# The first part of a down projection as seven products, moved into the gate-up stage

## The chip, the cores and the metric

The kernel runs on one NeuronCore of one Trainium2 chip. Such a core has a matrix engine (TensorE, PE in the profile; its weight loads are shown apart as PEld) and three engines for elementwise work: VectorE (DVE), ScalarE (ACT) and GpSimd (POOL). SyncE (SP) issues the DMA transfers. Each engine works through its own list of instructions in order and waits on semaphores for the others. SBUF is the memory on the chip with 128 partitions; PSUM takes the results of matmuls, in banks.

The metric is the device time of one execution in microseconds. The time before is 1231.87 us, the median of three runs (1230.77 to 1232.3).

## The reference, cut to what matters

Two layers work on 512 prompt positions and 64 sample positions, 576 columns in all, of model width 1024. The first mixes tokens by a convolution module, the second by stick-breaking attention. After each stands the same feed-forward block:

```python
D_FF = -(-8 * D_MODEL // (3 * 256)) * 256          # 2816 = 22 tiles of 128

def swiglu(xn, w_gu, w_down):
    g, u = jnp.split(xn @ w_gu, 2, axis=-1)
    return (jax.nn.silu(g) * u) @ w_down

    h = h + mix                                    # or the attention's output
    h = h + swiglu(rmsnorm(h, ffn_norm_g[l]), ffn_w_gu[l], ffn_w_down[l])
```

All is in float32. The outputs are the normalised stream, the convolution's states, and the keys and values.

## The kernel before, in words

**Products in three matmuls.** Each float32 operand is split into a high part in a rounded format and a low part (the rest). A product is made of three matmuls into one PSUM bank: high by high, high by low, low by high. The 576 columns are worked on as two halves of 288, so the unit of PE's work is a matmul of 128x128 weights with 128x288 operands.

**Weights.** A raw weight tile comes by DMA into one of four places (`wr0` to `wr3`). ACT writes its high part (`wh`) and also a copy of that in a PSUM bank (`hp`), and DVE subtracts that copy from the weights to get the low part (`wl`, L520). A piece has at most 512 columns, that is four blocks of 128, and lives in one of six slots (`N_W`). A slot comes free when its last matmul is done.

**Seven products for eight.** Most of the block is computed two output tiles at a time, in the Strassen-Winograd manner: two output tiles, the two halves of the contraction and the two halves of the columns make a 2x2 by 2x2 block product, for which seven block products are enough. `fast` lists the weights for it as seven pieces: 1, 2 and 4 are raw blocks, 7, 6, 5 and 3 are sums of raw blocks, made by POOL into one of four places `S` (L440 and L476; 5 is made on the way to 6 and used as a piece too). `operands` (L1318 on) makes the other side: for each pair of contraction tiles four sums (`ta`: L1357, L1360; `tb`: L1364, L1367), by the engines in `T_ENG`, and the high (ACT L1335) and low (DVE L1339) parts of these and of the raw halves. In the names, `('a', 0, 1)_2_tb` is layer 0, part 1, pair of columns 2, second sums. `run_jobs` issues the products (PE L1424) in the order of `FAST` = 7, 1, 6, 4, 2, 5, 3 for two pairs of output tiles at once, into three PSUM banks for each (A, B, C). After each product a piece of result is taken out of the bank.

**The feed-forward block** (`ffn`) has 22 tiles of the inner width. Gate-up: tile 0 is computed plainly, tile 1 by seven products alone, and tiles 2 to 21 in pairs, each pair by `run_jobs` over the normalised input's operands (`xops`). What comes out is copied by ACT (L1572) or added by DVE (L1578); POOL scales both results (L1601), ACT takes silu (L1605) and DVE multiplies (L1607). That leaves the tile `a`. Down: the contraction over 22 tiles is cut into three parts, `DK` = tiles 0 to 5, 6 to 13, 14 to 21, each added to the residual `h`. The first part is plain: `plain_operands` splits six tiles `a` (ACT L1626, DVE L1630), and for eight output tiles twelve products each run in `pd` (L596, `add_h` L751). The second and third part are seven-product jobs over `PAIRS` of output tiles, with operands from `a_operands`, and DVE adds each piece of result to `h` (L1693).

**What sets the order.** Nothing of this is written out in the order in which it runs. Each step is handed to a `Plan` as an operation with its engine, its cost and the tiles that it reads and writes. For each section of the program a list scheduler then places all operations on the engines, by the longest chain of work behind each, and the result of several rounds back and forth with the shortest end is emitted. Operations on POOL, and those on DVE that are marked `port` (both inputs in SBUF), are placed so that they don't overlap. A whole feed-forward block is one section. `prepare_operands` hands on the operands' steps one tile at a time, as long as there are places for them in SBUF (`spots`: `x` places, 36 `f` places and a few `k` places); `give` returns a place.

Of the kernel before, what the change touches and what calls it, by code (L numbers as in the profile page):

```python
# [3 lines left out]
F32 = mybir.dt.float32  # L4
# [84 lines left out]
DK = ((0, 6), (6, 14), (14, 22))  # L89
PAIRS = ((0, 4), (1, 5), (2, 6), (3, 7))  # L90
# [13 lines left out]
T_ENG = ("Pool", "Pool", "Pool", "Pool")  # L104
# [115 lines left out]
def build(tc, xT, vec, st, stp, bdp, wt, ck, cv, w_in, w_out, gu, down, wk, wv, wq, wo, yT, csp, css, kp, ks, vp, vs):  # L220
# [45 lines left out]
    def ffn_srcs(l):  # L266
# [1039 lines left out]
    def spot_tile(key, tag, dt=F32):  # L1306
        return tile(key, tag, (P, T), dt, pool=xpool if tag[0] == "x" else None)
# [151 lines left out]
    def ffn(l, mixer, g_next, nrm_next, x_busy, k_busy):  # L1459
# [153 lines left out]
        atags, adeps = [], {}  # L1613

        def plain_operands():

            for m in range(*DK[0]):
                yield 2
                tags_ = [single(), single()]
                atags.extend(tags_)  # L1620
                k = ("ap", l, m)

                def hi(m=m, k=k, tags_=tags_):
                    X[("at", l, m)] = ts = [spot_tile(k + (q,), t, F32R) for q, t in enumerate(tags_)]
                    X[k] = by_half(ts)
                    nc.scalar.activation(ts[0], X[("a", l, m)], AF.Copy)  # L1626

                def lo(m=m):
                    a, b = X[("at", l, m)]
                    nc.vector.tensor_tensor(b, X[("a", l, m)], a.bitcast(F32), op=ALU.subtract)  # L1630

                keys = [by_part(t) for t in tags_]
                op("ACT", act(T, False), hi, reads=by_part(at[m]), writes=keys[0] + keys[1])
                op("DVE", dve(T), lo, reads=by_part(at[m]) + keys[0], writes=keys[1], port=True)
                adeps[k] = keys[0] + keys[1]
                give(at[m])
# [38 lines left out]
        for m in range(2, NF, 2):  # L1675
            evacs = []
            finish = [gate_up(q, evacs) for q in (m, m + 1)]
# [3 lines left out]
            run_jobs(xops, evacs, m == NF - 2)  # L1681
            for f in finish:
                f()
        prepare_operands(force=True)
        table("natural_log_exp_and_others")

# [15 lines left out]
        for g in range(3):  # L1702
            if g < 2:
                a_operands(g + 1)
            if not g:
                for i, m in enumerate(ORDER):
                    tag = (("b0", "b1"), ("b2", "b3"), ("b4", "b5"))[i % 3]
                    prepare_operands()
                    wi, k = take(), ("pd", l, m, 0)
                    newps(k, tag)  # L1710
                    mm_ops(k, tag, wi, [("ap", l, q) for q in range(*DK[0])], xdeps=adeps.get)
                    add_h(m, k, tag)
                for t in atags:
                    give(t)
            for prs in (PAIRS[:2], PAIRS[2:]) if g else ():
# [755 lines left out]
```

## Time and profile before

One execution was profiled. Its span is 1229.2 us, while the timed runs gave 1230.77 to 1232.3 us.

| What | Value |
|---|---|
| timed runs, median | 1231.87 us |
| profiled execution, span | 1229.2 us |
| PE busy | 1204.8 us (98%), 8934 instructions in the trace |
| DVE busy | 978.2 us (80%) |
| ACT busy | 980.3 us (80%) |
| POOL busy | 766.2 us (62%) |
| HBM read | 105.18 MB |
| seven-product work on PE (L1424) in the chain of waits | 29% (A), 14% (B), 7% (C) of the span |
| `pd` (L596), the plain first part, in the chain of waits | 7% |

How to read it: an engine's busy time is the time in which it had an instruction under way. The chain of waits goes back from the last instruction to what released it, step by step, and says on which engine the span was spent. In groups of instructions a row shows line, engine, operation, the tile written and the tiles read, the shapes and the count, and then busy time in us and the mean length of one in ns; behind that comes the idle time ahead of them and what ended it. The first parts lie at about 463 to 505 us (layer 0) and 1087 to 1126 us (layer 1).

### The profile page before, as it was taken

The page shows a single profiled execution, that of the slowest core. Times are in us where ns is not written, and L with a number is a line of the kernel's source. Part 1 is how long each engine was busy: PE and PEld are TensorE (multiplying, and loading weights), DVE is VectorE, ACT ScalarE, POOL GpSimd, SP SyncE. Part 2 cuts the span into 40 slices and gives each one's busy share as a digit, 9 for nine tenths or more (in the row PEclk, how much of TensorE's full clock was granted, in tenths as well). Part 3 has the DMA queues.
Part 4 walks back from the last instruction along what each step waited for, and adds up shares of the span by engine and source line. Part 5 has one row for each costly group of instructions (what it writes and reads, how often), then busy time and mean ns, then how long its engine had stood idle before and what let it go on. Part 6 is the DMA issues. An engine that isn't in the chain of part 4 may idle for free.

```text
span 1229.2 us, 24245 instructions
## 1 busy us (share of the span) xinstructions
PE 1204.8 (98%) x8934; PEld 1185.0 (96%) x8934; DVE 978.2 (80%) x1599; ACT 980.3 (80%) x1877; POOL 766.2 (62%) x636
## 2 busy tenths in 40 slices
PE   9999989999999999999999999998999999999996
PEld 8999989999999999999999999998999999999996
DVE  6999977967665569886788999999866566699965
ACT  7998475698887888687678999956988888896873
POOL 1999824469767758855214555554877768677631
PEclk9999999999999999999999999999999999999999
DMA  7233822133232333223372232232232232332222
GB/s 270 86 93 97 263 71 73 52 115 93 87 121 69 104 86 104 87 82 106 111 202 62 52 83 65 53 103 69 70 123 84 87 119 71 98 108 83 92 69 78
DMA packets 44999, 121.10 MB, mean 99 GB/s; under 512 B 8784, under 2 KB 14224, under 8 KB 44880
## 3 DMA queue, kind: packets, MB, share of 16 engines
q1 hardware_dynamic: 44880, 119.56, 32.3%
q8 instruction: 70, 1.15, 0.4%
q14 instruction: 49, 0.40, 0.1%
HBM read 105.18 MB, written 5.70 MB: 90 GB/s over the span
## 4 chain that ended last, share of the span: by engine, by line
PE 81%; DVE 8%; ACT 1%; issue 1%; DMA 0%; POOL 0%; DVEq 0%; ACTq 0%
PE j_A L1424 29%; PE j_B L1424 14%; PE pd L596 7%; PE j_C L1424 7%; PE pq L596 4%; PE b L2206 4%; PE po L596 4%; PE pw L596 2%; PE b L2142 2%; PE b L2234 2%; DVE acc L1057 2%; PE pg L596 1%; PE pv L1957 1%; DVE wl L520 1%; PE pk L596 1%; DVE xs L1524 1%
## 5 line engine op out<-in xcount | busy, mean ns | idle before, releaser
L510 ACT ACTIVATE wh<-wr 128x512 fp32r<-128x512 f32 (+1 forms) x303 | 183.8, 612 | 36.9 <-PE po L596 15.2
L520 DVE TENSOR_TENSOR wl<-wr,hp 128x512 fp32r<-128x512 f32 (+1 forms) x241 | 158.6, 662 | 53.1 <-ACT hp L515 52.1
L520 DVE TENSOR_TENSOR wl<-S,hp 128x512 fp32r<-128x512 f32 x226 | 152.4, 680 | 40.6 <-ACT hp L515 37.7
L510 ACT ACTIVATE wh<-S 128x512 fp32r<-128x512 f32 x228 | 141.2, 627 | 31.9 <-PE pd L596 10.5
L515 ACT ACTIVATE hp<-wr 128x512 fp32r<-128x512 f32 (+1 forms) x241 | 139.0, 579 | 24.5 <-DVE wl L520 21.7
L515 ACT ACTIVATE hp<-S 128x512 fp32r<-128x512 f32 x226 | 134.0, 596 | 11.9 <-POOL S L440 6.9
L440 POOL TENSOR_TENSOR S<-wr,wr 128x512 f32<-128x512 f32 x57 | 76.5, 1341 | 93.0 <-ACT wh L510 31.0
L1074 POOL TENSOR_TENSOR pacc<-pacc,pr 128x608 f32<-128x608 f32 x69 | 108.9, 1592 | 7.9 <-ACT pr L1071 4.7
L476 POOL TENSOR_TENSOR S<-wr,S 128x512 f32<-128x512 f32 x57 | 78.8, 1385 | 30.2 <-DVE wl L520 17.3
L440 POOL TENSOR_TENSOR S<-wr 128x512 f32<-128x512 f32 x57 | 78.0, 1370 | 26.9 <-DVE wl L520 9.6
L440 POOL TENSOR_TENSOR S<-S,wr 128x512 f32<-128x512 f32 x57 | 77.2, 1354 | 14.4 <-DVE wl L520 7.1
L1601 POOL TENSOR_TENSOR a<-a,r 128x576 f32<-128x576 f32 x44 | 66.8, 1521 | 15.7 <-DVE a L1578 15.7
L1601 POOL TENSOR_TENSOR t<-t,r 128x576 f32<-128x576 f32 x44 | 65.8, 1497 | 9.4 <-ACT t L1572 8.1
L596 PE MATMUL pd<-ap,wh 128*128 128x288 f32 x384 | 66.0, 294 | 0.0
L1057 DVE SCALAR_TENSOR_TENSOR acc<-u,vecs,acc 128x608 f32<-128x608 f32 x76 | 64.5, 849 | 1.0
L1071 ACT ACTIVATE pr<-u,vecs 128x608 f32<-128x608 f32 x69 | 54.2, 797 | 8.1 <-POOL pacc L1074 7.8
L1607 DVE TENSOR_TENSOR a<-a,t 128x576 f32<-128x576 f32 x44 | 49.6, 1127 | 9.0 <-ACT t L1605 8.5
L596 PEld LDWEIGHTS pd<-ap,wh 128*128 128x128 f32 x384 | 56.0, 188 | 0.0
L520 DVE TENSOR_TENSOR wl<-wr,wh 128x512 fp32r<-128x512 f32 x62 | 49.7, 812 | 6.4 <-ACT wh L510 6.3
L1572 ACT ACTIVATE t<-j_A 128x288 f32<-128x288 f32 x84 | 34.0, 406 | 22.3 <-PE j_A L1424 21.5
L1693 DVE TENSOR_TENSOR h<-j_A,h 128x288 f32<-128x288 f32 x60 | 27.1, 453 | 19.6 <-PE j_A L1424 19.3
L1578 DVE TENSOR_TENSOR t<-j_C,t 128x288 f32<-128x288 f32 x42 | 19.1, 455 | 29.0 <-PE j_C L1424 28.9
(857 smaller groups left out, 4504.7 us busy)
## 6 DMA issues: line engine op xcount, KB each, us to landing
wr<-gu SPq DMA_DIRECT2D x88, 512.0 KB, 3.6
wr<-down SPq DMA_DIRECT2D x32, 512.0 KB, 3.7
wr<-w_in SPq DMA_DIRECT2D x15, 512.0 KB, 3.7
wm<-wt SPq DMA_DIRECT2D x12, 576.0 KB, 5.4
wr<-down SPq DMA_DIRECT2D x16, 384.0 KB, 3.2
qd<-qd SPq DMA_DIRECT2D x21, 256.0 KB, 3.0
wr<-w_out SPq DMA_DIRECT2D x8, 512.0 KB, 3.6
wr<-wq SPq DMA_DIRECT2D x8, 512.0 KB, 3.7
```

The source lines that it names most:

```text
L440: eng(e).tensor_tensor(t[:, :n], x[1](), y[1](), op=ALU.subtract if sub else ALU.add)
L476: eng(e).tensor_tensor(v[:, :n], X[("raw", i0)][:, n : 2 * n], v[:, :n], op=ALU.subtract)
L510: nc.scalar.activation(X[("w", u)][0][:, :n], get(), AF.Copy)
L515: nc.scalar.activation(t[:, :n], get(), AF.Copy)
L520: eng(le).tensor_tensor(b[:, :n], get(), a.bitcast(F32)[:, :n], op=ALU.subtract)
L596: nc.tensor.matmul(o[hf], (hi, hi, lo)[j][:, s], (xh, xl, xh)[j], start=(start and q == 0 and j == 0), stop=(stop and q == n - 1 and j == ...
L1057: nc.vector.scalar_tensor_tensor(dst, src, wt_, dst if i else X[("kneg",)], op0=ALU.mult, op1=ALU.add)
L1071: nc.scalar.activation(tile(("pr", c, i), f"pr{m}", (P, YW)), src, AF.Copy, scale=wt)
L1074: nc.gpsimd.tensor_tensor(X[("pacc", c)], X[("pacc", c)], X[("pr", c, i)], op=ALU.add)
L1424: nc.tensor.matmul(out, a[:, s], b, start=(start and q == 0 and i == 0), stop=(q == len(ops_) - 1 and i == 2), skip_group_check=True,)
L1601: nc.gpsimd.tensor_tensor(X[k], X[k], r, op=ALU.mult)
L1607: op("DVE", dve(T), lambda: nc.vector.tensor_tensor(X[ku], X[ku], X[kg], op=ALU.mult), reads=by_part(tg), writes=by_part(tu), port=True)
```

## The change

The down projection's first part is computed as seven products for two output tiles at a time, like the other two parts. It no longer stands behind the gate-up stage: when the pair of tiles 8 and 9 is done (`MID` = 10), the operands of tiles 0 to 5 are made, with their sums on DVE for this part, and the part's four pairs of output tiles follow, ahead of gate-up tiles 10 and 11. The weights' loads move with it in the list of sources. The plain path (`plain_operands`, the loop over `pd`) is gone. From tile 18 on (`AHEAD`), the operands of the second part are handed on between the gate-up pairs, as far as a reserve of places allows (two, and one more for each tile that is still to come). `down_evac` and `finished` only stand earlier.

```diff
+MID = 10
+AHEAD = 18
-T_ENG = ("Pool", "Pool", "Pool", "Pool")
+T_ENG = (("DVE", "DVE", "DVE", "DVE"), ("Pool", "Pool", "Pool", "Pool"), ("Pool", "Pool", "Pool", "Pool"))
...
         for m in range(2, NF, 2):
+            if m == MID:
+                a, b = DK[0]
+                for prs in PAIRS[:2], PAIRS[2:]:
+                    fast([[down[l, q][:, a * P : b * P] for q in p] for p in prs], (b - a) // 2)
             fast([(gu[l, q], gu[l, q + NF]) for q in (m, m + 1)], 4)
-        a, b = DK[0]
-        for m in ORDER:
-            direct(down[l, m][:, a * P : b * P], (b - a) * P)
...
-        def plain_operands():
...
-            todo_.append((operands(aops[g], ("a", l, g), ts, T_ENG, ("xf", "xf", "fx")[g], l == 1 and g == 2), 0))
+            todo_.append((operands(aops[g], ("a", l, g), ts, T_ENG[g], ("fx", "xf", "fx")[g], l == 1 and g == 2), 0))
...
         for m in range(2, NF, 2):
+            if m == MID:
+                a_operands(0)
+                prepare_operands(force=True)
+                for prs in PAIRS[:2], PAIRS[2:]:
+                    run_jobs(aops[0], [down_evac(p) for p in prs], prs == PAIRS[2:])
             evacs = []
             finish = [gate_up(q, evacs) for q in (m, m + 1)]
-            if m == NF - 2:
-                todo_.append((plain_operands(), 0))
-                prepare_operands()
+            if m == AHEAD:
+                a_operands(1)
+            if m >= AHEAD:
+                prepare_operands(2 + NF - 2 - m)
             run_jobs(xops, evacs, m == NF - 2)
             for f in finish:
                 f()
...
-        for g in range(3):
+        for g in (1, 2):
             if g < 2:
                 a_operands(g + 1)
-            if not g:
-                for i, m in enumerate(ORDER):
-                    tag = (("b0", "b1"), ("b2", "b3"), ("b4", "b5"))[i % 3]
-                    prepare_operands()
-                    wi, k = take(), ("pd", l, m, 0)
-                    newps(k, tag)
-                    mm_ops(k, tag, wi, [("ap", l, q) for q in range(*DK[0])], xdeps=adeps.get)
-                    add_h(m, k, tag)
-                for t in atags:
-                    give(t)
-            for prs in (PAIRS[:2], PAIRS[2:]) if g else ():
+            for prs in (PAIRS[:2], PAIRS[2:]):
```

Three places show how the instructions stand. In the rows a number behind a name tells the buffers of one name apart; lines of the changed kernel are 3 higher than before.

On PE before, in layer 0, where the last gate-up products end and the plain first part begins:

```order
L1424 MATMUL j_A<-('x', 0, 3)_0_b_1_2800,wh_5964 128x288
L1424 MATMUL j_A<-('x', 0, 3)_0_b_0_2799,wl_5965 128x288
L596 MATMUL pd_0_0_0_6047<-ap_0_0_5295,wh_5984 128x288
L596 MATMUL pd_0_0_1_6048<-ap_0_0_5295,wh_5984 128x288
L596 MATMUL pd_0_0_0_6047<-ap_0_1_5296,wh_5984 128x288
L596 MATMUL pd_0_0_1_6048<-ap_0_1_5296,wh_5984 128x288
```

On PE after the change, in layer 0, where the pair of tiles 8 and 9 ends:

```order
L1427 MATMUL j_A<-('x', 0, 3)_0_b_1_2731,wh_4155 128x288
L1427 MATMUL j_A<-('x', 0, 3)_0_b_0_2730,wl_4156 128x288
L1427 MATMUL j_B<-('a', 0, 0)_0_b_0_3586,wh_4183 128x288
L1427 MATMUL j_B<-('a', 0, 0)_0_b_1_3587,wh_4183 128x288
L1427 MATMUL j_B<-('a', 0, 0)_0_b_0_3586,wl_4184 128x288
L1427 MATMUL j_B<-('a', 0, 0)_1_b_0_3807,wh_4183 128x288
```

The first part stands in the middle of gate-up and in bank B of a job, with three matmuls for each pair of columns, one half of 288 each.

On POOL before, in layer 0, around the last pair of gate-up: the sums of the second part's operands, with only the scales by `r` between them.

```order
L1357 TENSOR_TENSOR ('a', 0, 1)_0_ta<-a_6_3640 128x288
L1357 TENSOR_TENSOR ('a', 0, 1)_1_ta<-a_7_3698 128x288
L1360 TENSOR_TENSOR ('a', 0, 1)_0_ta<-a_10_4260,a_6_3640 128x288
L1360 TENSOR_TENSOR ('a', 0, 1)_1_ta<-a_11_4316,a_7_3698 128x288
L1601 TENSOR_TENSOR t_0_20_5799<-t_0_20_5799,r 128x576
L1357 TENSOR_TENSOR ('a', 0, 1)_2_ta<-a_8_3954 128x288
L1364 TENSOR_TENSOR ('a', 0, 1)_0_tb<-a_10_4260,('a', 0, 1)_0_ta 128x288
L1360 TENSOR_TENSOR ('a', 0, 1)_2_ta<-a_12_4566,a_8_3954 128x288
L1357 TENSOR_TENSOR ('a', 0, 1)_3_ta<-a_9_4010 128x288
L1367 TENSOR_TENSOR ('a', 0, 1)_0_tb<-a_10_4260,('a', 0, 1)_0_tb 128x288
```

On POOL after the change, in the same place of layer 0:

```order
L443 TENSOR_TENSOR S_6_6402<-S_5_6266,wr_6165 128x512
L1360 TENSOR_TENSOR ('a', 0, 1)_2_ta<-a_8_3970 128x288
L1363 TENSOR_TENSOR ('a', 0, 1)_2_ta<-a_12_5147,a_8_3970 128x288
L479 TENSOR_TENSOR S_6_6402<-wr_6165,S_6_6402 128x512
L1367 TENSOR_TENSOR ('a', 0, 1)_2_tb<-a_12_5147,('a', 0, 1)_2_ta 128x288
L443 TENSOR_TENSOR S_7_6540<-wr_6413,wr_6465 128x512
L1360 TENSOR_TENSOR ('a', 0, 1)_3_ta<-a_9_4057 128x288
L1370 TENSOR_TENSOR ('a', 0, 1)_2_tb<-a_12_5147,('a', 0, 1)_2_tb 128x288
L1363 TENSOR_TENSOR ('a', 0, 1)_3_ta<-a_13_5224,a_9_4057 128x288
L1367 TENSOR_TENSOR ('a', 0, 1)_3_tb<-a_13_5224,('a', 0, 1)_3_ta 128x288
```

The sums of pairs of columns 2 and 3 now stand between sums of the weights (`S_6`, `S_7`, of 512); those of 0 and 1 stand earlier in the list.

On ACT after the change, a little later in layer 0:

```order
L1338 ACTIVATE ('a', 0, 1)_2_b_0_6600<-('a', 0, 1)_2_tb 128x576
L1575 ACTIVATE a_21_6482<-j_A 128x288
L1338 ACTIVATE ('a', 0, 1)_3_b_0_6614<-('a', 0, 1)_3_ta 128x576
L513 ACTIVATE wh_6592<-S_7_6540 128x512
L518 ACTIVATE hp_6633<-wr_6413 128x512
L518 ACTIVATE hp_6640<-S_6_6402 128x512
L1575 ACTIVATE t_0_20_6430<-j_A 128x288
```

The second part's operands are split among the weight pieces and the results of gate-up's last tiles.

More of the change, by code (lines that the diff above doesn't have):

```diff
@@ L1612, in ffn @@
         aops = [[], [], []]
-        atags, adeps = [], {}
-        def plain_operands():
[L1617 to L1636, printed above, removed]
         def a_operands(g):
@@ L1674, in ffn @@
         finish()
-        for m in range(2, NF, 2):
-            evacs = []
-            finish = [gate_up(q, evacs) for q in (m, m + 1)]
-            if m == NF - 2:
-                todo_.append((plain_operands(), 0))
-                prepare_operands()
[L1681 to L1685, printed above, removed]
         def down_evac(pair):
@@ L1700, in finished @@
                 out_gain(m)
[L1702 removed]
+        for m in range(2, NF, 2):
+            if m == MID:
[3 more added lines that the diff above has]
+                    run_jobs(aops[0], [down_evac(p) for p in prs], prs == PAIRS[2:])
+            evacs = []
+            finish = [gate_up(q, evacs) for q in (m, m + 1)]
+            if m == AHEAD:
+                a_operands(1)
+            if m >= AHEAD:
+                prepare_operands(2 + NF - 2 - m)
+            run_jobs(xops, evacs, m == NF - 2)
+            for f in finish:
+                f()
+        prepare_operands(force=True)
+        table("natural_log_exp_and_others")
+        for g in (1, 2):
             if g < 2:
                 a_operands(g + 1)
[L1705 to L1715 removed]
+            for prs in (PAIRS[:2], PAIRS[2:]):
                 if l == 1 and g == 2 and prs == PAIRS[2:]:
```

## The prediction

> **What bounds the kernel now.** I read the page's head first, then the chain of waits, then busy time in windows around the two feed-forward blocks, then what TensorE (PE) waited for in the second block's window.
>
> ```profile
> span 1229.2 us, 24245 instructions
> PE 1204.8 (98%) x8934; PEld 1185.0 (96%) x8934; DVE 978.2 (80%) x1599; ACT 980.3 (80%) x1877; POOL 766.2 (62%) x636
> PE 81%; DVE 8%; ACT 1%; issue 1%; DMA 0%; POOL 0%; DVEq 0%; ACTq 0%
> 418.00:590.00 172.00, 172.00 (x1298) 172.00 (x1297) 134.18 (x224) 136.70 (x262) 112.19 (x91) 1.00 0.30 90
> 1042.00:1204.00 162.00, 162.00 (x1229) 162.00 (x1228) 134.27 (x221) 132.77 (x259) 101.05 (x83) 1.00 0.28 85
> PE j_A L1424 <- ACT wh L510: 0.6, 1, 0.6
> ```
>
> PE is busy 98% of the span and 81% of the chain. The two window rows (length, then busy time and count of PE, weight loads, DVE, ACT and POOL, granted clock, DMA share, GB/s) hold the end of gate-up and the whole down projection of layers 0 and 1: PE has not a microsecond idle at full clock, while the others have 22% (DVE), 21% (ACT) and 35% (POOL) free. The last row is the only PE wait from 860 us to 1204 us. So a matmul taken away here is worth its whole pitch, and side work is free while it stays ahead of PE. The median 1231.87 us is 2.7 us above the profiled span; I carry those along unchanged.
>
> **Term 1, the matmuls.** The first part (six columns of 128, eight output tiles, two halves, three matmuls each) is 288 matmuls per layer now. As seven products over three column pairs for four tile pairs it is 7 x 3 x 3 x 4 = 252. 36 go per layer, 72 in all.
>
> ```profile
> L596 PE MATMUL pd<-ap,wh 128*128 128x288 f32 x384 | 66.0, 294 | 0.0
> L596 PE MATMUL pd<-ap,wl 128*128 128x288 f32 x192 | 40.8, 294 | 0.0
> 442.45 1.60 PE j_B L1424 x12
> 469.52 35.20 PE pd L596 x264
> ```
>
> The counts 384 + 192 confirm 576 for both layers, all 128x288. The 294 ns is latency; the pitch is 172.00 / 1298 = 132.5 ns by the window, 35.20 / 264 = 133.3 ns by the chain's plain piece, 1.60 / 12 = 133 ns by a seven-product piece (so the new kind is no slower). **72 x 0.1325 = -9.5 us.**
>
> The Trainium skill, "TensorE: Matmul & The Clock Gate", section "Back-to-back issue gap", gives N/2.4 + 2.5 ns for an isolated warm matmul. As an estimate that is 122.5 ns here, and 8.8 us; the rows say 132.5, and I keep theirs.
>
> **Term 2, side work: what is added.** The first part's weights now go as 28 pieces of 384 elements per layer (7 products x 4 pairs), where they were 8 of 512 and 8 of 256, and 16 sums of 384 on POOL come first.
>
> ```profile
> 901.28 0.61 ACT L515 ACTIVATE hp<-S 128x512 fp32r<-128x512 f32 x1
> 901.81 0.64 ACT L510 ACTIVATE wh<-S 128x512 fp32r<-128x512 f32 x1
> 902.33 0.61 ACT L515 ACTIVATE hp<-S 128x512 fp32r<-128x512 f32 x1
> L515 ACT ACTIVATE hp<-wr 128x256 fp32r<-128x256 f32 x16 | 6.0, 372 | 0.0
> L510 ACT ACTIVATE wh<-wr 128x256 fp32r<-128x256 f32 x16 | 6.5, 406 | 0.8 <-PE pd L596 0.6
> L2102 ACT ACTIVATE ze<-zt 128x384 fp32r<-128x384 f32 x16 | 8.4, 527 | 0.3 <-PE b L2234 0.3
> L1626 ACT ACTIVATE ap<-a 128x576 fp32r<-128x576 f32 x12 | 7.8, 679 | 0.0
> L520 DVE TENSOR_TENSOR wl<-S,hp 128x512 fp32r<-128x512 f32 x226 | 152.4, 680 | 40.6 <-ACT hp L515 37.7 <-PE pd L596 1.3 <-issue 0.5
> L520 DVE TENSOR_TENSOR wl<-wr,hp 128x256 fp32r<-128x256 f32 x16 | 6.5, 408 | 0.0
> L1693 DVE TENSOR_TENSOR h<-j_A,h 128x288 f32<-128x288 f32 x60 | 27.1, 453 | 19.6 <-PE j_A L1424 19.3
> L1630 DVE TENSOR_TENSOR ap<-a,ap 128x576 fp32r<-128x576 f32 x12 | 11.9, 1000 | 0.3 <-ACT ap L1626 0.3
> L440 POOL TENSOR_TENSOR S<-wr 128x512 f32<-128x512 f32 x10 | 13.0, 1298 | 3.6 <-ACT wh L510 2.2 <-DVE wl L520 1.5
> ```
>
> ACT's ops overlap by some 0.1 us: lengths of 0.61 start 0.52 apart. So 512 costs 0.52 us, 256 about 0.29, 384 about 0.42 (527 - 100), 576 about 0.58. Weights: 8 x 2 x (0.52 + 0.29) = 13.0 becomes 28 x 2 x 0.42 = 23.5. Operands: 6 x 0.58 = 3.5 becomes nine of 576 and three of 288, 6.1. ACT +13.1 us per layer.
> DVE, taken 0.08 off each length in the same way: low parts of weights 8 x (0.60 + 0.33) = 7.4 becomes 28 x 0.465 = 13.0; evacuations of 0.37 go from 16 to 28, +4.4; operands' low parts +3.1; their twelve sums of 288, on DVE for this group, 12 x 0.37 = 4.4. DVE +17.5 us per layer.
> POOL: 16 sums of 384, at 0.95 between its 512 (1.25 by pace) and its 288 below: +15.2 us per layer.
> SP: no load more, 16 of 384 KB only move ahead of 24 gate-up loads in its queue. They land in 3.2 us by the page's list and a pair of them feeds 63 matmuls, 8.3 us, so I cost the move at nothing.
>
> **Where it lies.** The first part now stands behind the pair of columns 8 and 9.
>
> ```profile
> 418.00:440.00 22.00, 22.00 (x168) 22.00 (x167) 13.15 (x22) 18.45 (x38) 16.10 (x13) 1.00 0.33 96
> 463.00:501.00 38.00, 38.00 (x288) 38.00 (x287) 35.85 (x55) 27.30 (x57) 29.58 (x26) 1.00 0.34 98
> 1087.00:1126.00 39.00, 39.00 (x302) 39.00 (x301) 38.96 (x57) 29.53 (x62) 32.35 (x28) 1.00 0.32 96
> ```
>
> The first row is one ordinary pair (168 matmuls). That pair and the first part together give PE 22.3 + 252 x 0.1325 = 55.7 us. Against it stand ACT 18.45 + 23.5 + 6.1 = 48.1 (86%), DVE 13.15 + 13.0 + 28 x 0.37 + 7.1 + 4.4 = 48.0 (86%), POOL 16.1 + 15.2 = 31.3 (56%). All fit, so I cost this place at nothing.
>
> The other two rows are the plain part's time. It is there that the second part's operands are made now, with DVE busy 35.85 of 38 and 38.96 of 39 us and PE still full: those 38 us are the cover that the change takes away. What was hidden there must go under the last two pairs and the second part itself. Without the plain part, the window 418 to 590 has 172 - 288 x 0.1325 = 133.8 us of PE for ACT 136.7 - 16.5 = 120.2 (90%), DVE 134.2 - 19.3 = 114.9 (86%; 7.4 + 6 x 1.0 + 16 x 0.37 taken off) and POOL at most 112.2 (84%). On average it fits; the question is the pile-up.
>
> ```profile
> 460.32 0.81 POOL L1357 TENSOR_TENSOR ('a', 0, 1)_0_ta<-a 128x288 f32<-128x288 f32 x1 [3.06 <-PE j_B L1424]
> 466.50 1.32 POOL L1364 TENSOR_TENSOR ('a', 0, 1)_0_tb<-a,('a', 0, 1)_0_ta 128x288 f32<-128x288 f32 x1
> 459.07 0.74 DVE L1630 TENSOR_TENSOR ap<-a,ap 128x576 fp32r<-128x576 f32 x1
> 465.80 1.36 DVE L1339 TENSOR_TENSOR ('a', 0, 1)_0_b<-('a', 0, 1)_0_ta,('a', 0, 1)_0_b 128x576 fp32r<-128x576 f32 x1
> ```
>
> The same operation takes 0.81 or 1.32 us on POOL, 0.74 or 1.36 on DVE: longer where a POOL instruction and a DVE one with both inputs in SBUF overlap. 1.32 us is one after the other, so I add the two as one resource.
> The Trainium skill, "SBUF — State Buffer", section "Who interferes with whom", says that such a pair shares a port that is locked for the whole instruction; the trace agrees (0.74 and 1.36).
>
> By the change's order I count this resource between the starts of weight-sum sets, each feeding 168 matmuls or 22.3 us of PE (layer 0). POOL is 1.25 per weight sum, 0.77 per operand sum, 1.40 per scale; DVE 0.67 per op of 576 and 0.37 per one of 288. From the last pair's set: 8 x 1.25 + 3 x 0.77 + 4 x 1.40 + 5 x 0.67 = 21.3, fits. From the second part's first set: 10 + 7 x 0.77 + 3 x 1.40 + 8 x 0.67 + 3 x 0.37 = 26.1, over by 3.8. From its second set: 10 + 10 x 0.77 + 1.40 + 7 x 0.67 + 0.37 = 24.2, over by 1.9. Lost per layer: nothing if what is in stock covers it, 5.7 us if nothing does. In stock are up to six weight slots of twelve matmuls, 6 x 1.60 = 9.6 us by the chain's row, and full slots at the start cover 5.7 easily. I take 1 us per layer, nearer to the free end since the rows with DVE at 38.96 of 39 show PE unharmed. **Term 2: +2 us, bounds 0 and +11.4.**
>
> The operands are ahead only in part: the order makes columns 0 and 1 of layer 0 (0 alone in layer 1) before the last pair, and the rest within it, since few places are free. The order also puts second-part products whose operands exist before the last gate-up products, so I add nothing for the start of the second part.
>
> **Sum.** -9.5 + 2.0 = -7.5: span 1221.7, time 1231.87 - 7.5 = **1224.4 us**. Its own range is 1221.5 (no stall, measurement noise 0.8) to 1227 (2.3 us per layer).
>
> **Rivals.**
> *The shared port takes half of it.* For it: the overruns of 3.8 and 1.9 come directly one after the other. Against it: slots in stock. At 3 us per layer: 1231.87 - 9.5 + 6 = 1228.4.
> *PSUM banks turn round too late.* Products 1 to 6 and 5 to 3 reuse a bank, and here only the other job's nine matmuls stand between, 1.19 us, not twelve, 1.60. Evacuation takes 0.45 plus what DVE is just doing (0.74, or 1.36). Against it: in most cases it fits. There are 16 such places; half of them at 0.6 give 4.8, beside the 2 us: 1229.2.
> *The operands aren't really ahead.* The second part's first product needs the sums of all four columns, made late and behind weight sums on POOL. The change then moves the wait to where gate-up meets the second part, 3 us per layer beside the 2: 1231.87 - 9.5 + 8 = 1230.4. Against it: products placed before.
> *Slower: the plain part was the cover.* The six slots aren't full when the operands come, since ACT is 90% and the port over 100%. Then all 5.7 per layer stand on PE, with 1.25 more for the slots' refilling (one weight sum): 2 x 6.95 = 13.9, less 9.5, is +4.4: 1236.3. It decides from 4.75 us of stall per layer on. For it: the quoted DVE rows of the cover, full. Against it: ACT's and DVE's 10% free over the window.
>
> **Chances.** My forecast 0.65, port half 0.13, banks 0.06, operands late 0.07, slower 0.09. A measurement of this kernel tells 0.2%, 2.5 us, from no change; that bound lies at 1229.4. Faster: 0.65 + 0.10 of the port case + 0.03 of the banks = 0.78. Within 0.2%: the rest of these two, the late operands = 0.13. Slower: 0.09. The range from 1221 to 1230.5 leaves out the slower case and the tails.
>
> **What would show it.** Right: 72 fewer matmul records; the pitch 132 ns; PE busy without a gap in both first parts, and less than 1.5 us of waits per layer between the last pair and the end of the second part, on ACT's weight pieces. Port rival: those waits at 3 us, with operations of 0.81 grown to 1.3 throughout the second part. Banks: PE waits on L1693's counterpart after products 1 and 5 of the first part. Late operands: one long wait at the second part's first product. The forecast is wrong if PE loses over 2.3 us per layer there, or anywhere else in the block, or if the pitch changes.

## The result and the profile after

The changed kernel takes 1224.88 us (median of four runs, 1223.93 to 1225.98), the kernel before in the same runs 1231.74 us (1230.77 to 1232.3). The ratio is 0.9946, with a 95% interval from 0.9931 to 0.9960: 6.9 us faster, where 7.5 were predicted (1224.4).

The head of the page of the profiled execution after, whose own time is 1224.83 us:

```profile
span 1222.9 us, 24388 instructions
PE 1198.5 (98%) x8862; PEld 1177.0 (96%) x8862; DVE 1023.8 (84%) x1683; ACT 1002.7 (82%) x1937; POOL 815.1 (67%) x668
PE 75%; DVE 12%; issue 1%; ACT 1%; POOL 1%; DMA 1%; DVEq 0%; POOLq 0%; ACTq 0%; SPq 0%
```

PE has 72 records less (8934 to 8862), all the others have more work, and in the chain of waits PE's share fell from 81 to 75% while DVE's rose from 8 to 12%. The span is 6.3 us shorter. To see where, I summed the distances from the start of each matmul to the start of the next, by the part to which the matmul belongs, both layers together:

| us, by PE starts | before | after | difference |
|---|---|---|---|
| gate-up by seven products | 470.2 | 468.7 | -1.5 |
| first part | 75.8 | 66.8 | -9.0 |
| second parts | 89.0 | 90.5 | +1.4 |
| third parts | 90.9 | 92.5 | +1.6 |
| from layer 0's last product to layer 1's gate-up | 242.3 | 243.1 | +0.9 |

The first part gives 9.0 us. 3.9 us go again, in the three last rows, and 1.5 come from the start of gate-up, which the change doesn't touch (two waits of 0.7 and 0.6 us that stood there before are gone).

Windows of after (length, then busy time and count of PE, weight loads, DVE, ACT and POOL, granted clock, DMA share, GB/s): the two first parts in their new place, then the second and the third part of layer 0, and of layer 1.

```profile
331.50:365.20 33.70, 33.60 (x254) 33.36 (x253) 29.82 (x63) 30.02 (x68) 22.17 (x20) 1.00 0.35 110
951.30:985.00 33.70, 33.70 (x257) 33.70 (x256) 30.58 (x65) 29.66 (x67) 21.90 (x20) 1.00 0.35 110
497.40:543.20 45.80, 45.20 (x338) 44.60 (x337) 44.39 (x74) 41.86 (x78) 43.77 (x34) 1.00 0.30 93
543.20:589.50 46.30, 46.30 (x350) 46.10 (x348) 37.18 (x66) 36.95 (x68) 27.52 (x27) 1.00 0.29 87
1116.80:1163.00 46.20, 46.20 (x350) 46.16 (x349) 44.97 (x74) 43.60 (x83) 46.20 (x36) 1.00 0.31 92
1163.00:1200.00 37.00, 36.13 (x270) 35.64 (x269) 33.51 (x59) 30.70 (x56) 15.76 (x13) 1.00 0.17 58
```

The moved first parts run almost without a gap, as costed. In the second parts DVE, ACT and POOL are all nearly full (44.4, 41.9 and 43.8 of 45.8 us in layer 0). Before, layer 0's second part had this window:

```profile
504.70:549.00 44.30, 44.30 (x337) 44.30 (x336) 38.24 (x68) 36.76 (x67) 32.01 (x29) 1.00 0.30 96
```

What PE's matmuls waited for in the changed kernel, from 340 to 592 us (layer 0) and from 860 us on (layer 1):

```profile
PE pk L599 <- ACT xh L736: 1.2, 1, 1.2
PE j_A L1427 <- DVE h L1660: 0.5, 1, 0.5
PE pk L599 <- DVE xl L740: 0.3, 1, 0.3
...
PE j_A L1427 <- DVE ('a', 1, 2)_3_b L1342: 0.7, 1, 0.7
PE j_A L1427 <- DVE h L1660: 0.2, 1, 0.2
```

None of these is a weight piece; a weight load waited for one at 508.74 us, for 0.27 us. DVE is late with two things: with emptying bank A (`h` from `j_A`) and with an operand's low part. ACT is late with the next stage's first split (`xh`). The longest wait for a bank, on DVE's and POOL's timeline (start, length, line, tiles) and then PE's:

```profile
518.06 1.59 DVE L1342 TENSOR_TENSOR ('a', 0, 2)_2_b<-a,('a', 0, 2)_2_b 128x288 fp32r<-128x288 f32 x1
521.13 0.87 DVE L1342 TENSOR_TENSOR ('a', 0, 2)_3_b<-a,('a', 0, 2)_3_b 128x288 fp32r<-128x288 f32 x1
521.93 0.44 DVE L1660 TENSOR_TENSOR h<-j_A,h 128x288 f32<-128x288 f32 x1
...
518.03 1.30 POOL L443 TENSOR_TENSOR S<-S,wr 128x512 f32<-128x512 f32 x1
520.39 1.30 POOL L443 TENSOR_TENSOR S<-wr 128x512 f32<-128x512 f32 x1 [1.05 <-DVE wl L523]
...
522.43 0.54 PE L1427 MATMUL j_A<-('a', 0, 1)_0_b,wh 128*128 128x288 f32 x2 [0.53 <-DVE h L1660]
```

Low parts of 288, which take 0.44 us alone, take 1.59 and 0.87 behind POOL's sums. They are operands of the third part, and the addition that empties the bank stands behind them in DVE's queue. By the order on PE, product 6 of this job follows its product 1 with one product (twelve matmuls) between.

The third loss is the hand-over to the keys and values stage. ACT's splits around the end of layer 0's block, whose last matmul starts at 593.49 us before:

```profile
588.54 0.76 ACT L733 ACTIVATE xh<-h,vecs 128x576 fp32r<-128x576 f32 x1
590.85 0.77 ACT L733 ACTIVATE xh<-h,vecs 128x576 fp32r<-128x576 f32 x1
593.61 0.77 ACT L733 ACTIVATE xh<-h,vecs 128x576 fp32r<-128x576 f32 x1
```

After, the last matmul starts at 589.46 us; ACT's rows, and then PE's first of the next stage:

```profile
579.16 0.78 ACT L736 ACTIVATE xh<-h,vecs 128x576 fp32r<-128x576 f32 x1 [1.25 <-DVE h L1660]
587.34 0.76 ACT L736 ACTIVATE xh<-h,vecs 128x576 fp32r<-128x576 f32 x1
590.09 3.43 ACT L736 ACTIVATE xh<-h,vecs 128x576 fp32r<-128x576 f32 x5
...
590.91 0.54 PE L599 MATMUL pk<-xh,wh 128*128 128x288 f32 x2 [1.15 <-ACT xh L736]
```

Both kernels have two splits of `h` ready in time. But before, the next stage's first matmul started at 593.75 us, ahead of the end of the third split (594.38), so it read one of these two; now it starts when the third ends (590.91 us), and ACT makes that one only behind the block's last matmul. This loss is thus a choice of the schedule; an experiment below shows that side work in the block has no part in it.

What did become of the cover: before, no low part of an operand was made inside layer 0's third part, and in the second part ten; after, six and fifteen. What the plain part used to cover is now done within the parts themselves.

### The profile page after: what moved, and what is told of

It reads as the page before. It is cut to its first block, busy times and chain, and to the rows that moved or that the text cites. A ratio compares the mean times of both kernels' runs of the same rounds, so it can differ in the third digit from the quotient of the medians.

```text
span 1222.9 us, 24388 instructions
## 1 busy us (share of the span) xinstructions
PE 1198.5 (98%) x8862; PEld 1177.0 (96%) x8862; DVE 1023.8 (84%) x1683; ACT 1002.7 (82%) x1937; POOL 815.1 (67%) x668
## 4 chain that ended last, share of the span: by engine, by line
PE 75%; DVE 12%; issue 1%; ACT 1%; POOL 1%; DMA 1%; DVEq 0%; POOLq 0%; ACTq 0%; SPq 0%
PE j_A L1427 29%; PE j_B L1427 14%; PE j_C L1427 7%; PE pq L599 4%; PE b L2181 4%; PE po L599 4%; DVE wl L523 2%; PE pw L599 2%; PE b L2117 2%; PE b L2209 2%; DVE acc L1060 2%; PE pv L1932 1%; DVE h L1660 1%; PE pk L599 1%; PE pd L599 1%
## 5 line engine op out<-in xcount | busy, mean ns | idle before, releaser
L523 DVE TENSOR_TENSOR wl<-S,hp 128x512 fp32r<-128x512 f32 (+1 forms) x258 | 169.6, 663 | 41.2 <-ACT hp L518 38.9
L513 ACT ACTIVATE wh<-S 128x512 fp32r<-128x512 f32 (+1 forms) x260 | 155.8, 610 | 7.2 <-PE j_C L1427 3.0
L518 ACT ACTIVATE hp<-S 128x512 fp32r<-128x512 f32 (+1 forms) x258 | 148.5, 580 | 12.1 <-DVE wl L523 6.5
L443 POOL TENSOR_TENSOR S<-wr,wr 128x512 f32<-128x512 f32 (+1 forms) x65 | 89.5, 1377 | 86.1 <-ACT wh L513 33.6
L479 POOL TENSOR_TENSOR S<-wr,S 128x512 f32<-128x512 f32 (+1 forms) x65 | 93.0, 1431 | 25.7 <-DVE wl L523 14.7
L443 POOL TENSOR_TENSOR S<-wr 128x512 f32<-128x512 f32 (+1 forms) x65 | 86.5, 1331 | 20.7 <-ACT wh L513 8.5
L443 POOL TENSOR_TENSOR S<-S,wr 128x512 f32<-128x512 f32 (+1 forms) x65 | 91.1, 1403 | 7.5 <-DVE wl L523 6.3
L2083 POOL TENSOR_TENSOR e<-t,e 128x512 fp32r<-128x512 f32 (+1 forms) x20 | 27.0, 1352 | 23.1 <-DVE e L2079 12.3
L2117 PE MATMUL b<-qd,kst 128*128 128x256 f32 (+2 forms) x168 | 38.3, 338 | 0.0
L2083 DVE TENSOR_TENSOR s<-t,s 128x512 fp32r<-128x512 f32 (+2 forms) x44 | 35.3, 812 | 3.6 <-ACT s L2077 3.1
```

The lines of the kernel that those rows point to most:

```text
L443: eng(e).tensor_tensor(t[:, :n], x[1](), y[1](), op=ALU.subtract if sub else ALU.add)
L479: eng(e).tensor_tensor(v[:, :n], X[("raw", i0)][:, n : 2 * n], v[:, :n], op=ALU.subtract)
L513: nc.scalar.activation(X[("w", u)][0][:, :n], get(), AF.Copy)
L518: nc.scalar.activation(t[:, :n], get(), AF.Copy)
L523: eng(le).tensor_tensor(b[:, :n], get(), a.bitcast(F32)[:, :n], op=ALU.subtract)
L2083: eng(le).tensor_tensor(q[:, 1, sl], X[tk][:, sl], q.bitcast(F32)[:, 0, sl], op=ALU.subtract)
```

## The experiments

All were compared with the kernel before on the same chip (its medians 1231.1 to 1231.8 us).

**The move alone.** The first part stays plain, in its new place:

```diff
-                for prs in PAIRS[:2], PAIRS[2:]:
-                    fast([[down[l, q][:, a * P : b * P] for q in p] for p in prs], (b - a) // 2)
+                for q in ORDER:
+                    direct(down[l, q][:, a * P : b * P], (b - a) * P)
...
-                a_operands(0)
+                todo_.append((plain_operands(), 0))
                 prepare_operands(force=True)
-                for prs in PAIRS[:2], PAIRS[2:]:
-                    run_jobs(aops[0], [down_evac(p) for p in prs], prs == PAIRS[2:])
+                for i, q in enumerate(ORDER):
+                    ...
+                    mm_ops(k, tag, wi, [("ap", l, c) for c in range(*DK[0])], xdeps=adeps.get)
+                    add_h(q, k, tag)
```

> The first part stays plain (288 matmuls per layer in pd, six tiles split without sums) but stands behind tiles 8 and 9, as in the change; the second part's operands are handed on ahead as in the change. No matmul is saved. Theory (the stall is the price of the cover that was moved away, and the change's gain is the 72 matmuls): the end of the block is as in the change, so PE loses some 3 us in the second and third parts of both layers (1.5 in layer 0, 1.6 in layer 1) and the time is 1231.7 + 3 = 1234.5 (1233 to 1236). Rival (the stall comes from the additional weight pieces, sums and evacuations of the seven products): without them no stall, 1231.7 within 1. Rival (the gain is in the move and not in the matmuls): 1225 to 1227.

Measured: 1234.19 us against 1231.54, ratio 1.0021 (1.0012 to 1.0029). The move without the seven products makes the kernel 2.65 us slower, and 9.3 us above the change, so that the gain is in the matmuls. The size was expected (1234.5), but not for the reason given. By PE's starts the second and third parts lose nothing (89.1 and 90.9 us), although DVE and POOL are as full there as in the change; the loss is at the hand-over, 244.5 us against 242.3. This is all that PE waited for from 470 to 640 us:

```profile
PE pk L599 <- ACT xh L736: 1.1, 1, 1.1
PE pk L599 <- DVE xl L740: 0.3, 1, 0.3
```

Windows of this kernel, the second part of layer 0 and then 3.3 us of the next stage, from 3.4 us behind the block's last matmul on:

```profile
502.00:547.00 45.00, 45.00 (x341) 45.00 (x340) 44.52 (x75) 42.20 (x78) 44.44 (x35) 1.00 0.31 94
...
596.70:600.00 3.30, 3.30 (x15) 3.30 (x15) 2.71 (x5) 3.30 (x7) 0.93 (x1) 0.50 0.87 332
```

The changed kernel's window at the same point of the next stage:

```profile
592.80:596.10 3.30, 3.30 (x27) 3.30 (x26) 2.71 (x5) 3.30 (x7) 0.88 (x1) 1.00 0.83 320
```

After the same two waits the changed kernel gets 27 matmuls done at full clock, and the plain one 15 at a clock of 0.50. So the hand-over costs 0.9 us in both, and 1.4 more where the clock fell. My theory, that the lost cover alone makes PE wait in the second and third parts, falls with this: a stretch as full as this can go without a wait.

**Seven products in the old place.** The first part isn't moved:

```diff
-            if m == MID:
-                a_operands(0)
...
             if m == AHEAD:
-                a_operands(1)
+                a_operands(0)
...
-        for g in (1, 2):
+        for g in (0, 1, 2):
```

> Seven products for the first part, but where the plain part stood, behind gate-up; its operands are handed on ahead from tile 18 on, and the second part's are made under it. Theory (72 matmuls of 0.1325 us are saved wherever it stands; the cover is here again, 33.4 us of it, but this stretch has the side work of the first part as well: ACT 137 + 13 and DVE 134 + 17 of 162 us, 92 and 93%): PE loses 3 to 6 us over both layers, 1226 to 1229. Rival (the move as such costs 3 us, and in place nothing is lost): 1222 to 1223. Rival (the move is what makes the seven products pay, since behind gate-up the side work doesn't fit): 1230 or more.

Measured: 1237.49 us, ratio 1.0051 (1.0037 to 1.0065): slower than before, 12.6 us slower than the change. The third reading holds. Windows of the first and second part of layer 0 and of the first of layer 1:

```profile
464.70:504.00 39.30, 36.05 (x266) 35.15 (x265) 38.32 (x72) 35.45 (x77) 37.17 (x33) 1.00 0.31 95
504.00:549.00 45.00, 44.24 (x327) 43.22 (x326) 44.91 (x80) 39.05 (x73) 42.78 (x36) 1.00 0.32 95
1091.00:1128.00 37.00, 33.21 (x245) 32.30 (x244) 37.00 (x67) 33.48 (x73) 34.84 (x30) 1.00 0.33 101
```

The longest of PE's waits there, three in layer 0 and two in layer 1:

```profile
PE j_A L1423 <- ACT wh L509: 0.9, 1, 0.9
PE j_B L1423 <- ACT wh L509: 0.9, 1, 0.9
PE j_C L1423 <- DVE ('a', 0, 0)_0_b L1338: 0.8, 1, 0.8
...
PE j_A L1423 <- DVE ('a', 1, 0)_1_b L1338: 2.1, 1, 2.1
PE j_A L1423 <- DVE ('a', 1, 0)_2_b L1338: 1.4, 1, 1.4
```

Two of the three in layer 0 are on ACT's weight pieces; those in layer 1 are on operands' low parts from DVE. DVE is 98 and 100% busy in the first parts, and PE loses 9.2 us in them and 4.9 in the second ones. Nine of the twelve sums and six (layer 0) or four (layer 1) of the twelve low parts are ready when the first part starts, and the first sum starts 14 us ahead; in the moved place all twelve sums and ten low parts are, and the first starts 68 us ahead in layer 0 and 62 in layer 1. The move is what lets the seven products keep their gain. My percentages (92 and 93% over 162 us) were too coarse for this: they averaged over a stretch that is full at its start.

**Operands not handed on ahead.**

```diff
-            if m == AHEAD:
-                a_operands(1)
-            if m >= AHEAD:
-                prepare_operands(2 + NF - 2 - m)
...
+        a_operands(1)
+        prepare_operands()
         for g in (1, 2):
```

> The change, with the second part's operands handed on only behind the last pair of gate-up (from tile 18 on nothing is handed on). Theory (in the change they come ahead only in part, two columns of four, and what counts is how much side work stands in the second part): the sums move 2 to 4 us later on POOL and more low parts stand in the second part, PE loses 2 to 4 us more than in the change: 1227 to 1229. Rival (the scheduler places the sums by their inputs anyway, and handing on ahead does nothing): 1224.9 within 1.

Measured: 1229.51 us, ratio 0.9981 (0.9972 to 0.9990). Handing on ahead is worth 4.6 us, more than expected; 13 and 11 of the sixteen sums are ready at the second parts' start, where the change has 16 and 14. The second parts take 4.0 us more than before (2.5 more than in the change), the third parts 1.2, and the hand-over 2.1, with the clock falling there as in the plain case.

**Another order of products, against the wait for bank A.**

```diff
+DOWN = (7, 1, 4, 6, 2, 5, 3)
...
-                run_jobs(aops[g], [down_evac(p) for p in prs], prs == PAIRS[2:])
+                run_jobs(aops[g], [down_evac(p) for p in prs], prs == PAIRS[2:], order=DOWN)
```

The second and third part got this order, with their weights; the first kept its own, although the expectation speaks of all three.

> The change, with the products of all three parts of the down projection in the order 7, 1, 4, 6, 2, 5, 3: product 6 then follows product 1 in bank A with three products between them and not one. Theory (about half of the stall is PE waiting for bank A to be emptied by DVE, which is late because of operations stretched by POOL): the waits of j_A on DVE's additions to h, 0.9 us for products 6 in layer 0 and 0.4 in layer 1, go away, and the time is 1223.5 (1223 to 1224.3). Rival (DVE is late with everything, and PE waits for the next thing instead, a low part of a weight or of an operand): 1224.9 within 0.6. Rival (what the other order does to the weight sums costs more): 1226 or more.

Measured: 1230.11 us, ratio 0.9984 (0.9970 to 0.9997). The waits for bank A are gone, as expected; one of 0.5 us for bank B is new in layer 1's third part, and most of the time is lost elsewhere. Windows of the second and third part of layer 0:

```profile
497.00:541.60 44.60, 44.60 (x338) 44.60 (x337) 41.95 (x71) 41.70 (x78) 44.21 (x35) 1.00 0.32 96
541.60:587.00 45.40, 45.40 (x345) 45.40 (x344) 37.42 (x67) 37.89 (x68) 25.54 (x20) 1.00 0.29 90
```

The longest wait from 330 to 640 us:

```profile
PE pk L600 <- ACT wh L514: 3.7, 1, 3.7
```

In layer 0 PE loses nothing in the parts (44.5 and 44.4 us for 336 matmuls each), and then waits 3.7 us for the first weight piece of the next stage. In this schedule ACT makes that piece behind five splits of `h`. Its runs scatter from 1226.31 to 1235.46 us, far more than the others; why, I can't say. The profiled execution took 1226.56 us, so what the median's further 3.6 us are isn't shown.

**Low parts left out, sums left out, and both.** The second and third parts' low parts aren't made (DVE; the matmuls read the high part in their place), or their sums aren't (POOL; the splits read plain halves):

```diff
-            op("DVE", dve(n), lo, reads=reads + hk, writes=lk, port=True)
+            if gk[0] != "a" or gk[2] == 0:
+                op("DVE", dve(n), lo, reads=reads + hk, writes=lk, port=True)
...
-            for e, (f, rd, wr) in zip(engs, lst):
+            for e, (f, rd, wr) in zip(engs, lst if gk[0] != "a" or gk[2] == 0 else ()):
```

> The change, but in the second and third parts the low parts of the operands are left out (DVE's 16 and 20 operations per part; the matmuls read the high part twice instead, so their number and size stay). Theory (what PE loses against the sum of matmuls, 1.4 us in the second parts, 1.6 in the third, 0.9 at the start of the keys and values stage, is side work that no plain part covers any more, and DVE is the engine that is late): nearly all of it comes back, 1222 (1221.2 to 1222.8). Rival (the late engine is ACT with its weight pieces, or POOL with its sums): still there, 1224.3 or more.

> The change, but in the second and third parts POOL's sums of operands are left out (32 of 288 per layer, some 25 us; the splits read the plain halves instead, so ACT, DVE and PE have the same operations). Theory (DVE is late partly because its operations with two inputs in SBUF are held up by POOL's, 1.36 us for 0.74): low parts come earlier and shorter, and most of the stall goes away, 1222.5 (1221.5 to 1223.5). Rival (POOL and DVE don't matter to each other here, DVE has too many operations by itself): 1224.3 or more.

> The change with both left out in the second and third parts: POOL's sums and DVE's low parts of the operands. What is left there of the operands' work is ACT's. Theory (the waits in these parts come from DVE's two-input operations and POOL's operations holding each other up, with an emptying of a bank behind them in DVE's queue): no wait of 0.2 us or more in second and third parts of either layer; what still lies over the sum of matmuls is then the start of the keys and values stage, 0.9 us, and the time is 1222.3 (1221.5 to 1223.3). Rival (ACT's weight pieces and its operand work are the limit, at 90% of the window): waits remain in the parts, 1224 or more.

Measured: 1225.29 us without low parts (0.9950, 0.9937 to 0.9964), 1224.15 without sums (0.9946, 0.9934 to 0.9959), 1221.03 without both (0.9917, 0.9903 to 0.9930). Neither of the two alone gives what I expected, and the first lies in its rival's band (1224.3 or more). Without the sums the second and third parts lose 1.2 us and no longer 3.1, but the hand-over takes 244.6 us, with the clock falling there as in the plain moved kernel. Without the low parts the third parts lose nothing, and neither does layer 1's second part to speak of (0.2 us), but layer 0's second part loses 4.3. On its timeline stand DVE's multiplication, POOL's rows beside it and PE's wait:

```profile
511.02 3.75 DVE L1613 TENSOR_TENSOR a<-a,t 128x576 f32<-128x576 f32 x1
...
511.32 0.81 POOL L1366 TENSOR_TENSOR ('a', 0, 2)_0_ta<-a,a 128x288 f32<-128x288 f32 x1
512.09 0.81 POOL L1363 TENSOR_TENSOR ('a', 0, 2)_1_ta<-a 128x288 f32<-128x288 f32 x1
512.86 1.29 POOL L443 TENSOR_TENSOR S<-wr 128x512 f32<-128x512 f32 x1
515.49 1.27 POOL L443 TENSOR_TENSOR S<-wr,wr 128x512 f32<-128x512 f32 x1 [1.34 <-DVE wl L523]
...
518.49 0.55 PE L1430 MATMUL j_A<-('a', 0, 1)_0_b,wh 128*128 128x288 f32 x1 [2.54 <-DVE h L1663]
```

Windows of the same kernel, the whole second part of layer 0 and the 2.5 us behind that wait:

```profile
498.00:543.00 45.00, 42.46 (x310) 42.26 (x309) 31.80 (x54) 40.88 (x78) 38.09 (x38) 0.96 0.31 95
...
518.50:521.00 2.50, 2.50 (x10) 2.50 (x11) 1.40 (x3) 2.50 (x7) 2.50 (x3) 0.50 0.02 7
```

DVE has only 31.8 of 45 us to do, and one multiplication of 0.74 us takes 3.75: POOL's operations follow one another without a pause, and it ends 0.6 us behind the third of them, when POOL at last has to wait for DVE. The bank's addition stands behind it and a second multiplication of 1.73 us, PE waits 2.5 us, and then the clock is 0.50 in the window of 2.5 us. So here it isn't the amount of DVE's work that makes it late, but the meeting of its two-input operations with a row of POOL's. Such a meeting needn't cost PE as much: in layer 1's second part one multiplication takes 3.56 us, and PE loses 0.2. The profiled execution, 1226.54 us, is the slowest of the five (fastest 1223.47), so the size of the loss is that of this execution. With both left out, the longest multiplication in the second parts takes 1.28 us, and the second parts of both layers have PE full while ACT, at 99% in each, has kept all its work (windows of that kernel):

```profile
497.00:541.70 44.70, 44.65 (x338) 44.45 (x337) 32.10 (x59) 44.09 (x83) 25.62 (x21) 1.00 0.32 95
1115.00:1159.00 44.00, 44.00 (x334) 44.00 (x333) 30.39 (x57) 43.63 (x85) 25.32 (x20) 1.00 0.31 97
```

That clears ACT for the second parts. One wait of 0.21 us for bank A remains by PE's starts, a little over the bound I had set, and 0.8 us at the hand-over stay, as expected: what is lost there doesn't come from this work. The time lies 0.5 us under the range I had put.

**Where the sums are made, and when.** These change constants alone:

```diff
-T_ENG = (("DVE", "DVE", "DVE", "DVE"), ("Pool", "Pool", "Pool", "Pool"), ("Pool", "Pool", "Pool", "Pool"))
+T_ENG = (("DVE", "DVE", "DVE", "DVE"), ("DVE", "DVE", "DVE", "DVE"), ("Pool", "Pool", "Pool", "Pool"))
...
-MID = 10
+MID = 8
...
-AHEAD = 18
+AHEAD = 16
```

The first edit puts the second part's sums on DVE; a variant of it puts the third part's there too. The second edit moves the first part by one pair of tiles. The third was run together with the first, and so was the second.

> The change, with the second part's 16 sums per layer on DVE (0.37 us each) and not on POOL (0.77). If the stall is set by POOL and DVE shutting each other out, the two together get 6.4 us shorter per layer, and the time falls to 1223.5 (1222.5 to 1224.3). If DVE's own count of operations sets it (5.9 us more per layer), it rises to 1226 or more. Within 0.6 of 1224.9: neither, or both cancel.

> The change, with the operand sums of all three parts on DVE (32 of 288 per layer at 0.37 us leave POOL, where they take 0.77). Theory (the shared time of POOL and DVE counts, not DVE's own): the third part gains as the second did, 1223.5 (1222.5 to 1224.3). Rival (DVE is then busy over 95% of the second and third parts, and its own queue is the limit): 1225 to 1227.

> The change with the first part one pair of gate-up tiles earlier (behind tiles 6 and 7). Nothing at the end of the block changes by design. Theory (the stall is a matter of the side work at the block's end): 1224.9 within 0.8. Rival (where each operation happens to be placed by the scheduler decides as much as the amount of work): outside of that, either way by 1 to 3 us.

> The second part's sums on DVE, and its operands handed on from tile 16 on (18 in the change). If what counts is how many of them are done before the second part starts, more columns come ahead and the time falls below that of the sums on DVE alone (1224.24): 1222.8 (1222 to 1223.8). If the places in SBUF decide (none is free any earlier), it stays within 0.7 of 1224.2.

> The first part one pair earlier (behind tiles 6 and 7) and the second part's sums on DVE: the two edits that came out at 1225.0 and 1224.24, the first of them with no wait over 0.2 us in the second and third parts, the second with none there in layer 0. If each takes its own waits away, both together give 1223.3 (1222.5 to 1224). If what is won depends on where the scheduler happens to put an operation, the sum of two good orders is no better than either: 1224 to 1227.

Measured: second part's sums on DVE 1224.24 us (0.9943, 0.9931 to 0.9955), which lies where the shared time of POOL and DVE would put it, but the interval covers the change's own; all on DVE 1227.48 (0.9967, 0.9955 to 0.9980), just above its rival's 1225 to 1227, with DVE at 46.30 of 47 us in layer 1's second part:

```profile
1118.00:1165.00 47.00, 46.09 (x339) 44.97 (x338) 46.30 (x83) 43.71 (x83) 29.61 (x20) 1.00 0.29 91
```

One pair earlier: 1225.00 (0.9953, 0.9940 to 0.9965), equal in time, but with no wait at all in the second and third parts and 2.2 us more than the change in gate-up and 1.5 in the first parts instead. Handed on from tile 16: 1231.23 (0.9996, 0.9987 to 1.0005), 6.5 us worse than the sums on DVE alone by the two ratios, where I had expected a gain or nothing. Sums on DVE with the first part earlier: 1228.37 (0.9972, 0.9960 to 0.9984), worse than either alone. What PE waited for in layer 0's second part, handed on from tile 16:

```profile
PE j_B L1427 <- DVE ('a', 0, 1)_3_b L1342: 1.1, 1, 1.1
PE j_A L1427 <- DVE ('a', 0, 1)_3_b L1342: 0.7, 1, 0.7
```

The longest wait in layer 1's gate-up, with sums on DVE and the first part earlier:

```profile
PE j_A L1427 <- DVE a L1581: 2.3, 1, 2.3
```

A window of that kernel around this wait:

```profile
900.00:920.00 20.00, 17.68 (x121) 17.37 (x120) 19.32 (x25) 14.84 (x32) 16.91 (x11) 0.91 0.11 32
```

In the first of these, twelve of the sixteen sums are ready at the second part's start, fewer than the fourteen with `AHEAD` = 18 and the sums on DVE, although they are handed on earlier; why the schedule comes out like that wasn't settled. In the second, one bank is emptied 2.3 us late, and the clock falls (the profiled execution, 1229.9 us, is its slowest of six). The same amount of work, placed differently by the scheduler, thus gives 1224 to 1231 us: no variant with all its work beats the change by more than the measurement tells.

## Why the prediction was right

**Term 1, -9.5 us: right.** The first parts' time fell by 9.0 us in the profile. (The change against the move alone gives 9.3, but that is by chance: the change has 3.1 us of waits in the later parts that the other hasn't, and is spared 1.4 of slow clock and 1.8 in gate-up.) The small difference is the plain part of layer 1, which had run at 130 ns per matmul (37.45 us for 288), and not at 132.5.

**The moved place at nothing: right.** 33.4 to 33.5 us for 252 matmuls, with DVE at 29.8 and ACT at 30.0 of 33.7 us. The prediction had not seen that this place is the condition of the gain. It asked what the move costs and never what the seven products would cost unmoved: 1237.49 us.

**Term 2, +2 us, bounds 0 and +11.4: the right size, by another way.** The second and third parts lost 3.1 us. The hand-over's 0.9 isn't in my sum at all, and the 1.5 us that came back at the start of gate-up aren't either. So it is partly luck that the time came within 0.6 us: the profile's 6.3 us are 9.0 - 3.1 - 0.9 + 1.5, and 0.2 lost elsewhere. The number of operations added is as costed (84 on DVE, 32 on POOL in both layers), but busy time rose by 45.6 us on DVE and 48.9 on POOL where I had 35.0 and 30.4: the operations got longer. The step that failed is the one that says what runs dry. I took the shared time of POOL and DVE as the resource, had it drain a stock of six weight slots, and named waits "on ACT's weight pieces" as the sign. No wait of over 0.3 us in these parts is one. The resource is borne out in part: leaving out both kinds of operation that meet there brings the parts back to the full pitch within 0.2 us, leaving out one kind doesn't, and the rows of 1.59 and 3.75 us show the meeting. But the runs don't separate it from DVE's own queue everywhere: with all sums on DVE the shared time is shorter still by my prices, and the time was 1227.48 us. And a late DVE hits PE sooner than through weights: through the bank that it empties, for which the stock in the PSUM bank is one product of 1.6 us, and through the low part of an operand.

**The rivals.** The shared port taking half: its mechanism is at work in the rows shown, its 3 us per layer were not reached (about 1.5). The banks: I put them into the first part, where nine matmuls stand between products; there PE lost 0.3 us at one place in layer 0 and nothing else. They turned up in the second part, where twelve matmuls are between, since DVE is full there. Late operands: 0.8 us in layer 1's third part, nothing at the second part's start. Slower: it didn't come; what late operands cost shows in the variants, 1229.5 without handing on ahead and 1237.5 without the move.

The Trainium skill, "SBUF — State Buffer", section "Who interferes with whom", says that the issue order decides which of the two blocks, and for the whole instruction. The 1.59 and 0.87 us rows agree. The row of 3.75 doesn't: by the recorded starts DVE's instruction began at 511.02 us and was passed by three of POOL's that began later (511.32, 512.09 and 512.86 us).

## What to carry to other kernels

A cheaper algorithm that trades matmuls for side work is worth its matmuls in a stretch where the engines beside PE have time to spare, and here only there: against the plain part in the same place, the same seven products gained 9.3 us in the middle of gate-up and lost 6 behind it. When a covering stretch is taken away, follow the covered work to where it is done now, and look first at PSUM banks, whose stock is one product, before the deeper stocks of weights. Average shares of 85 to 90% say little: which instruction stands behind which in a queue decided over several microseconds in either direction.

## What the hardware showed that I had not expected

*A starved DVE operation.* One multiplication of 0.74 us took 3.75 us while POOL ran its operations back to back; 1.36 was the most I had counted with, and 2.04 the longest of these multiplications before.

*Short waits cost clock.* After PE idled 2.54 us (the kernel without low parts) the granted clock was 0.50, and the next thirteen matmuls stood 0.24 us apart instead of 0.1325: 1.4 us more. The same followed an idle of about 1.1 and 0.3 us close together in the plain moved kernel, while the changed kernel with the same two waits kept a clock of 1.00. The Trainium skill, "TensorE: Matmul & The Clock Gate", section "HAM oscillation — how this bites in real kernels", puts the bound at idle gaps over about 3.4 us; the runs here show the half clock after 2.5 us, and after less in some executions. The clock records of the traces show what differed. Inside the kernels every stretch at half clock lasts 3.41 us, and where a trace has two, their starts lie a whole number of such lengths apart (163.1 and 596.6 us in the plain moved kernel, 127 of them). On this grid both waits of the plain moved kernel fall into one slot, from 593.2 to 596.6 us, with 1.48 us idle in all, and the next slot is the slow one; in the changed kernel a border of the grid at 591.2 us parts them into 1.16 and 0.32 us. How much idle time in a slot it takes isn't settled: the kernel without sums and low parts kept its clock with 1.48 us in one. A wait of 2.5 us was thus worth 3.9, and this is one reason why schedules with the same work lie so far apart.
